# A hybrid encoder layer on one core: the opening in another order

## The chip, the core and the metric

The kernel runs on one core of a Trainium2 chip. The metric is the time of one execution on the device in microseconds (us), the median of several runs. A core has five engines with a queue each: PE (TensorE: matmuls and transposes, weight loads shown as PEld), DVE (VectorE), ACT (ScalarE), POOL (GpSimd) and SP (SyncE, which here issues all transfers). Each works its own list in order and waits on semaphores. PE writes into PSUM, eight banks of 128 x 512 floats, from which only DVE and ACT read here.

## The reference

One encoder layer on x of 1024 tokens by 1024 channels, conditioned by a vector c:

```
mod = silu(c) @ w_ada + b_ada          # six rows of 1024: sh1, sc1, gt1, sh2, sc2, gt2
h = rms_norm(x, g_norm1) * (1 + sc1) + sh1
qa, ka, va, qb, kb, vb, gates = split(h @ w_in)
o_a = neighbourhood_attention(rms_norm(qa), rms_norm(ka), va, rpb)        # 8 heads
o_b = merge of three dilated_window_attentions of rotary(rms_norm(qb)), rotary(rms_norm(kb)), vb
x = x + gt1 * ((sig(gate_a) * (o_a @ w_proj_a) + sig(gate_b) * (o_b @ w_proj_b)) @ w_o)
h2 = rms_norm(x, g_norm2) * (1 + sc2) + sh2
x = x + gt2 * ((silu(a) * up) @ w_ffn_out),   a, up = split(h2 @ w_ffn_in)
```

All data are float32. The change lies in the first two lines and the first part of the third.

## The kernel before, in words

**Split products.** A float32 matrix is kept as two parts, `hi` (rounded by an ACT copy, L101 for weights) and `lo` (the difference, on POOL or DVE, L102). A product is three matmuls, hi by hi, hi by lo and lo by hi (`PASS`). `wsplit` makes the two parts of a weight tile from a landed `raw` tile.

**The opening** (L142 to L729) has its order written out by hand for all engines: what stands first in the program goes first on each engine. It makes hT, the transposed and modulated h, in two parts of eight channel blocks k (128 channels each) by 1024 tokens, and the first six token tiles of the projection of unit 0. Its pieces:

- x is loaded in eight token tiles (L148, 512 KB each). `x_squares`, `x_rstd` and `x_scale` normalise tile t; for tiles 0 to 3 the scale sits in a diagonal matrix and `x_turn` transposes by a plain matmul (L207), for tiles 4 to 7 x itself is scaled and `x_turn` is a PE transpose (L209). Each `x_turn(t)` fills two PSUM banks, of the pair `d`, `v` or `s` by t modulo 3. `x_evac(t)` copies them to yT on DVE or ACT (L216, L218), as a table `XE` says.
- `load_block(k)` loads 1 MB of w_ada, the two columns blocks of sc1 and sh1 for channel block k, in two halves (`land`, L155); `unit_load(0, k)` loads unit 0's weights of block k (`raw`, L94). `start_load(k)` does both.
- `ada_rows(k)` multiplies c by that block on PE (L619) and asks for block k + 3 by `start_load(k + 3)`; `rowk[k]()` copies the row to SBUF on ACT (L625); `ada_turn(k)` turns it into columns on PE (L634); `ada_cols(k)` adds gains and biases on DVE (L639, L641).
- `h_half(k, hf)` makes one token half of block k of hT: a scale and shift on DVE (L647), hi on ACT (L648), lo on DVE (L651). With half 0 it also splits unit 0's weights of block k (`wsplit`, hi on ACT, lo on POOL).
- the loop at the end of the opening goes over k: `start_chunk(k, (0, 1, 2))` (nine matmuls, L656), `ada_turn`, `ada_cols` and both halves for block k + 2, `start_chunk(k, (3, 4, 5))`, then `ada_rows(k + 3)` and `rowk[k + 3]`.

Tables are asked for on SP's queue too: `rg` (L238) and the mask `bm` (L240) right behind x, then `cs` (L229) in `new_unit(0)`. From `rg` and `cs` POOL makes the rotary table `rtab` (L233, four operations), which stand on POOL ahead of the first weight split. Behind these, in the program, come the first three `start_load`.

**The main loop** goes over n, from 6 to 91; n = 8u + t is token tile t of unit u (of ten units, each a pair of heads). PE's order is by hand through the whole kernel; outside the opening a planner with a timeline of its own sets the order on the other engines. In iteration n PE does four of the tile's eight chunks (24 matmuls in all, L281), scores of attention items, products with v (`at_pv`, a `v` bank, copied by DVE at L476), turns (`qk_turn`: transposes of q and k, L339, with copies L357 to L360 on ACT and DVE), turns of the attention weights, and the other four chunks; for n below 10 all eight chunks come first. Then `proj_post` normalises q and k (ACT L299, L300; the copy of v at L316). The list `turns` says which tiles of unit 0 are turned in iterations 8 to 11; from 10 on, one tile of the tile two iterations before is turned as well. Turns of iterations 8 and 9 use the `s` banks, later ones the `v` banks. There are two banks of each kind.

The rest (gates, merge, output projection, feed-forward) isn't touched.

Of the kernel before, what the change touches and what calls it, by code (L numbers as in the profile page):

```python
# [35 lines left out]
def hybrid_layer(ctx: ExitStack, tc: tile.TileContext, x, colp, wada1, wada2, bada2, wqkv, wg, wpa, wpb,  # L36
# [21 lines left out]
    def bank(tag):  # L58
        return ps.tile([128, 512], F32, tag=tag, name="ps_" + tag)
# [29 lines left out]
    def fview(ap):  # L89
        return ap.bitcast(F32)  # L90
# [6 lines left out]
    def wsplit(r, eng=None):  # L97
        n = r.shape[1]
        hi = wp.tile([128, 512], F32R, tag="hi", bufs=NHL, name="whi")
        lo = wp.tile([128, 512], F32R, tag="lo", bufs=NHL, name="wlo")  # L100
        nc.scalar.activation(hi[:, :n], r, AF.Copy)  # L101
        (eng or nc.gpsimd).tensor_sub(lo[:, :n], r, fview(hi[:, :n]))  # L102
        return hi, lo
# [48 lines left out]
    def load_block(k):  # L152
        wblk[k] = [landing().rearrange("p (k n) -> p k n", k=4) for _ in range(2)]
        for hf in range(2):
            nc.sync.dma_start(wblk[k][hf], wada1[k, :, hf * 4:hf * 4 + 4, :])  # L155

    def unit_load(u, k):
        return wload(wqkv[u, :, k, :], 384)
# [3 lines left out]
    def start_load(k):  # L162
        if k < KT:
            load_block(k)
            raw0.append(unit_load(0, k))

    pw = bank("t")
    for i in range(WARM):
        nc.tensor.transpose(pw[:, :128], ident, ident)
# [2 lines left out]
    def x_squares(t):  # L172
        p, i = divmod(t, 2)
        if i == 0:
            ss2[p] = ap_.tile([128, 2], F32, tag="ss2", bufs=2, name="ss2")
        acc, junk = ss2[p][:, i:i + 1], hT[0][:, t, :]
        if XSQ[t] == "a":
            nc.scalar.activation(junk, xts[t], AF.Square, accum_out=acc)
        else:
            nc.vector.tensor_tensor_reduce(junk, xts[t], xts[t], 1.0, 0.0, ALU.mult, ALU.add, acc)  # L180
# [11 lines left out]
    def x_scale(t):  # L192

        r = xr[t // 2][:, t % 2:t % 2 + 1]
        if XSC[t] == "d":
            xd[t] = ap_.tile([128, 128], F32, tag="stg", bufs=3, name="xd")
            nc.vector.tensor_scalar(xd[t], ident, r, None, op0=ALU.mult)
        else:
            nc.vector.tensor_scalar(xts[t], xts[t], r, None, op0=ALU.mult)

    def x_turn(t):
        for g in range(2):
            pt = xp[t, g] = bank("dvs"[t % 3])
            for i in range(4):
                src, dst = xts[t][:, (g * 4 + i) * 128:(g * 4 + i + 1) * 128], pt[:, i * 128:(i + 1) * 128]
                if XSC[t] == "d":
                    nc.tensor.matmul(dst, src, xd[t], start=True, stop=True)  # L207
                else:
                    nc.tensor.transpose(dst, src, ident)  # L209

    def x_evac(t, gs=(0, 1)):
        for g in gs:
            dst = yT[g][:, :, t * 128:(t + 1) * 128]
            src = xp[t, g].rearrange("p (k q) -> p k q", k=4)
            if XE[t][g] == "v":
                nc.vector.tensor_copy(dst, src)  # L216
            else:
                nc.scalar.activation(dst, src, AF.Copy)  # L218
# [57 lines left out]
    def proj_chunk(U, t, k):  # L276
        if k == 0:
            U.pd[t] = bank("d" if U.u else "t")
        pd = U.pd[t]
        for i, (a, b) in enumerate(PASS):  # L280
            nc.tensor.matmul(pd[:, :384], tok(a, k, t), U.w[k][b][:, :384],  # L281
                             start=(k == 0 and i == 0), stop=(k == KT - 1 and i == 2))
# [321 lines left out]
    units = []  # L604
# [5 lines left out]
    rowk = {}  # L610

    def ada_rows(k):

        if k >= KT:
            return
        pa = bank("t")
        for kk in range(8):
            j = 32 * (kk % 4)
            nc.tensor.matmul(pa[j:j + 32, :256], c32[:, kk, :], wblk[k][kk // 4][:, kk % 4, :],  # L619
                             start=(kk < 4), stop=(kk >= 4))  # L620
        start_load(k + 3)

        def copy():
            rowk[k] = ap_.tile([128, 384], F32, tag="p", bufs=4, name="rowk")[:, :256]
            nc.scalar.activation(rowk[k], pa[:, :256], AF.Copy)  # L625

        rowk[k] = copy
# [3 lines left out]
    def ada_turn(k):  # L631
        ps_m = sck[k] = bank("t")
        for i in range(2):
            nc.tensor.matmul(ps_m[:, i:i + 1], rowk[k][:, i * 128:i * 128 + 128], ones, start=True, stop=True)  # L634

    def ada_cols(k):
        ps_m = sck[k]
        sc = sck[k] = ap_.tile([128, 2], F32, tag="sc", bufs=3, name="sc")
        nc.vector.scalar_tensor_tensor(sc[:, 0:1], ps_m[:, 0:1], g1_c[:, k:k + 1], bg1[:, k:k + 1],  # L639
                                       op0=ALU.mult, op1=ALU.add)  # L640
        nc.vector.tensor_add(sc[:, 1:2], ps_m[:, 1:2], bsh1[:, k:k + 1])  # L641

    def h_half(k, hf):
        sc = sck[k]
        hs = slice(hf * 512, hf * 512 + 512)
        y = yT[k // 4][:, k % 4, hs]
        nc.vector.tensor_scalar(y, y, sc[:, 0:1], sc[:, 1:2], op0=ALU.mult, op1=ALU.add)  # L647
        nc.scalar.activation(hT[0][:, k, hs], y, AF.Copy)  # L648
        if hf == 0:
            w0.append(wsplit(raw0[k]))  # L650
        nc.vector.tensor_sub(hT[1][:, k, hs], y, fview(hT[0][:, k, hs]))  # L651
# [4 lines left out]
                nc.tensor.matmul(U.pd[t][:, :384], tok(a, k, t), U.w[k][b][:, :384],  # L656
                                 start=(k == 0 and i == 0), stop=(k == KT - 1 and i == 2))

    for k in range(3):
        start_load(k)  # L660
    x_squares(0)
    x_squares(1)
    x_rstd(0)
# [9 lines left out]
    x_scale(3)  # L673
    x_turn(2)
    x_turn(3)
    ada_rows(0)
    x_squares(4)
    x_squares(5)
    x_evac(0, (1,))
# [8 lines left out]
    x_rstd(3)  # L688
    x_scale(6)
    x_scale(7)  # L690
    rowk[0]()
    x_evac(2)
    x_evac(3)
    x_turn(5)
    ada_turn(0)
    ada_rows(1)
    x_turn(6)
    x_evac(4)
    x_turn(7)
    rowk[1]()  # L700
    ada_cols(0)
    xp_.release()
    h1l = pool("h1l", "left")
    hT.append(h1l.tile([128, KT, S], F32R, name="hT1"))
    x_evac(5)
    h_half(0, 0)
    x_evac(6)
    x_evac(7)
    h_half(0, 1)
    ada_turn(1)  # L710
    ada_rows(2)
    ada_cols(1)
    h_half(1, 0)
    h_half(1, 1)
    rowk[2]()
    for tg, t in zip(["d", "d", "s", "s", "v", "v"], range(6)):
        U.pd[t] = bank(tg)
    for k in range(KT):
# [17 lines left out]
    for n in range(6, 92):  # L736
        u, t = divmod(n, 8)
        if u < 10:
            if t == 0:
                units.append(new_unit(u, [nextw[u, k] for k in range(KT)]))  # L740
            U = units[u]
            chunks = [lambda k=k, U=U, t=t: proj_chunk(U, t, k) for k in range(KT)]
        elif n - 80 < NPRE:
            chunks = gate_pre(n - 80)
        else:
            chunks = []
        if u + 1 < 10:
            for k in ([0, 1, 2, 3, 4, 5, 6, 7] if n == 6 else [t] if u else []):
                raws[u + 1, k] = unit_load(u + 1, k)
            if t == 6:  # L750
                for k in range(2):
                    nextw[u + 1, k] = wsplit(raws[u + 1, k])
        if t == 2 and 1 <= u <= 10:
            for slot, I in unit_items(units[u - 1]):
                ready.setdefault(8 * u + 2 + slot, []).append(I)
        if n == 8 * 7 + 5:
            combine_stats()
        ci = n - (8 * 7 + 7)
        if 0 <= ci < 12:
            combine_prep(ci)  # L760
        done, prev, cur = prev, cur, ready.pop(n, [])

        def chunk():
            if chunks:
                chunks.pop(0)()
                k = 8 - len(chunks)
                if t == 7 and u + 1 < 10 and k < 8 and k >= 2:
                    nextw[u + 1, k] = wsplit(raws[u + 1, k], nc.vector if k % 2 else None)

        turns = [(units[0], tt) for tt in {8: (0, 1, 2), 9: (3, 4, 5), 10: (6,), 11: (7,)}.get(n, ())]  # L770
        if 10 <= n <= 81:
            turns.append((units[(n - 2) // 8], (n - 2) % 8))
        chunk()
        chunk()
        chunk()
        chunk()
        if n < 10:
            while chunks:
                chunk()
        for I in cur:  # L780
            at_scores(I)
            at_qk(I, 0)
            at_qk(I, 1)
        for I in done:
            at_pv(I)
        for q in turns:
            qk_turn(*q, "s" if n < 10 else "v")
        for I in prev:
            at_turn(I, 0)
            at_turn(I, 1)  # L790
        chunk()
        chunk()
        chunk()
        chunk()
        if n >= 8 and (t != 7 or u > 8) and ada_state["i"] < 65:
            ada_step()
        if 1 <= ci < 13:
            combine_step(ci - 1)
        while chunks:
            chunk()  # L800
        if u < 10:
            proj_post(U, t)
# [516 lines left out]
```

## Time and profile before

| | us |
|---|---|
| median of 3 runs | 1610.39 |
| lowest and highest run | 1608.18 and 1611.52 |
| the profiled execution | 1611.13 |
| its span, first to last instruction | 1609.3 |

The span is what the profile divides: all times below count from its start. Of the profiled execution 1.8 us lie outside it. The mean granted TensorE clock was 0.984. The views used are the page (busy time by engine, the chain of work that ended last), the timeline of an engine (start, duration, engine, line, operation, tiles, count, and in brackets how long the engine had been idle and which work ended that), and the windows (busy time of each engine in given stretches, with clock and DMA).

### The profile page before, as it was taken

The numbers are of one execution on the slowest core, as the hardware profiler recorded it, in microseconds if no ns is written. First come the engines' busy times: TensorE is split into PE (matmuls) and PEld (weight loads), VectorE is DVE, ScalarE is ACT, GpSimd is POOL, SyncE is SP. The second block draws the span as 40 slices with busy tenths as digits, with TensorE's granted clock in tenths as the row PEclk, the third lists the DMA queues.
The fourth block names the chain that finished last, engine by engine and source line by source line (L and its number), as shares of the span: only waits on it lengthen the run. The fifth ranks groups of instructions, "written<-read, shape, count | busy, mean of one in ns | idle before, by whom it ended". The sixth has DMA issues, their size and how long they took to land.

```text
span 1609.3 us, 24779 instructions
## 1 busy us (share of the span) xinstructions
PE 1549.1 (96%) x8240; PEld 1293.8 (80%) x8240; DVE 1026.0 (64%) x2188; ACT 667.0 (41%) x1734; POOL 719.5 (45%) x672
## 2 busy tenths in 40 slices
PE   7989999999999999999999986999999999999997
PEld 6888888898888877878887775788888888888886
DVE  5666666776889843352437979866666666345476
ACT  5555555555545443512124533323233333344442
POOL 1332321221101040645425576867766666555565
PEclk8999999999999999999999998999999999999999
DMA  8332331344344351776645521333333333576774
GB/s 316 105 119 58 102 110 49 119 133 113 91 133 127 91 172 57 257 236 218 216 152 183 176 93 40 102 111 102 108 109 99 105 98 120 178 232 193 249 216 166
DMA packets 149056, 227.52 MB, mean 141 GB/s; under 512 B 27312, under 2 KB 65072, under 8 KB 148928
## 3 DMA queue, kind: packets, MB, share of 16 engines
q1 hardware_dynamic: 148928, 225.94, 44.1%
q8 instruction: 65, 1.06, 0.3%
q14 instruction: 63, 0.52, 0.1%
HBM read 172.28 MB, written 53.59 MB: 140 GB/s over the span
## 4 chain that ended last, share of the span: by engine, by line
PE 76%; DVE 11%; DMA 5%; issue 3%; ACT 2%; POOL 2%; SPq 0%; POOLq 0%; DVEq 0%; ACTq 0%
PE ps_d L281 14%; PE ps_t L1059 6%; PE ps_v L1059 6%; PE ps_s L1059 6%; PE ps_d L1059 6%; PE ps_d L570 4%; PE ps_d L592 4%; PE ps_s L570 4%; PE ps_d L1161 3%; PE ps_s L1161 3%; PE ps_v L473 2%; PE ps_s L432 2%; PE ps_v L1161 2%; PE ps_t L1161 2%; PE ps_t L570 2%
## 5 line engine op out<-in xcount | busy, mean ns | idle before, releaser
L102 POOL TENSOR_TENSOR wlo<-raw,whi 128x512 fp32r<-128x512 f32 (+2 forms) x269 | 362.2, 1354 | 474.9 <-ACT whi L101 455.4
L101 ACT ACTIVATE whi<-raw 128x512 fp32r<-128x512 f32 (+2 forms) x418 | 244.1, 604 | 431.3 <-DMA raw<-in_wg_dram 69.7
L281 PE MATMUL ps_d<-whi,hT 128*128 128x384 f32 x1152 | 317.9, 344 | 0.0
L102 DVE TENSOR_TENSOR wlo<-raw,whi 128x512 fp32r<-128x512 f32 (+1 forms) x149 | 150.5, 1019 | 129.0 <-ACT whi L101 114.9
L281 PEld LDWEIGHTS ps_d<-whi,hT 128*128 128x128 f32 x1152 | 211.2, 189 | 5.5 <-ACT vs L319 3.5
L281 PE MATMUL ps_d<-wlo,hT 128*128 128x384 f32 x576 | 194.2, 337 | 0.8 <-POOL wlo L102 0.8
L281 PEld LDWEIGHTS ps_d<-wlo,hT 128*128 128x128 f32 x576 | 108.9, 189 | 1.5 <-POOL wlo L102 1.5
L311 POOL TENSOR_TENSOR ra<-qn,rtab 128x64 f32<-128x64 f32 x48 | 16.5, 344 | 166.6 <-DVE qn L304 122.8
L996 POOL TENSOR_TENSOR c<-c 128x512 f32<-128x512 f32 x40 | 64.6, 1617 | 51.8 <-DVE c L1109 45.5
L101 ACT ACTIVATE whi<-ws 128x512 fp32r<-128x512 f32 x60 | 37.9, 632 | 117.1 <-DVE ws L1069 34.4
L447 ACT ACTIVATE P<-P,st 128x256 f32<-128x256 f32 (+2 forms) x100 | 46.3, 463 | 69.8 <-DVE st L446 69.8
L1059 PE MATMUL ps_t<-t,whi 128*128 128x512 f32 x160 | 52.6, 410 | 13.3 <-DVE c L995 12.1
L302 DVE TENSOR_REDUCE ss<-sq 128x4 f32<-128x256 f32 x80 | 33.2, 415 | 47.7 <-ACT sq L299 47.5
L447 ACT ACTIVATE P<-P,sx 128x384 f32<-128x384 f32 (+1 forms) x64 | 37.1, 580 | 51.6 <-DVE sx L446 51.6
L473 PE MATMUL ps_v<-PT,v 128*64 128x128 f32 (+1 forms) x672 | 55.0, 284 | 1.6 <-DVE PT L462 1.6
L458 PE MATMUL ps_t<-ident,P 128*128 128x128 f32 (+1 forms) x336 | 51.8, 275 | 4.3 <-DVE P L450 1.8
L432 PE MATMUL ps_s<-qk 64*128 64x256 f32 (+3 forms) x492 | 53.7, 321 | 2.2 <-DVE st L446 1.6
L592 PE MATMUL ps_d<-hT,whi 128*128 128x512 f32 x176 | 55.5, 396 | 0.0
L995 DVE TENSOR_TENSOR c<-c 128x512 f32<-128x512 f32 x40 | 45.5, 1139 | 14.2 <-ACT c L994 14.2
L570 PE MATMUL ps_s<-hT,whi 128*128 128x512 f32 x176 | 54.4, 390 | 0.0
L432 PEld LDWEIGHTS ps_s<-qk 64*128 64x128 f32 (+1 forms) x492 | 35.0, 182 | 24.0 <-issue 11.5
L876 DVE TENSOR_TENSOR raw<-raw 128x512 f32<-128x512 f32 x11 | 7.8, 708 | 70.9 <-DMA raw<-in_w_dram 51.4
(360 smaller groups left out, 4052.2 us busy)
## 6 DMA issues: line engine op xcount, KB each, us to landing
raw<-in_w_dram SPq DMA_DIRECT2D x165, 256.0 KB
ga_d<-c SPq DMA_DIRECT2D x77, 256.0 KB
raw<-ga_d SPq DMA_DIRECT2D x77, 256.0 KB
wa<-in_wada_dram SPq DMA_DIRECT2D x32, 512.0 KB
raw<-in_wqkv_dram SPq DMA_DIRECT2D x80, 192.0 KB
raw<-in_wo_dram SPq DMA_DIRECT2D x48, 256.0 KB
w_d<-raw SPq DMA_DIRECT2D x44, 256.0 KB
raw<-w_d SPq DMA_DIRECT2D x44, 256.0 KB
```

The source lines that it names most:

```text
L101: nc.scalar.activation(hi[:, :n], r, AF.Copy)
L102: (eng or nc.gpsimd).tensor_sub(lo[:, :n], r, fview(hi[:, :n]))
L281: nc.tensor.matmul(pd[:, :384], tok(a, k, t), U.w[k][b][:, :384], start=(k == 0 and i == 0), stop=(k == KT - 1 and i == 2))
L432: nc.tensor.matmul(I.pS[h][:nq, :nk], U.qk[a][hs, I.q0:I.q0 + nq], U.qk[2 + b][hs, I.kb0 * 128:I.kb0 * 128 + nk], start=(i == 0), stop=(i ...
L447: nc.scalar.activation(P[:nq, :nk], P[:nq, :nk], AF.Exp, scale=-1.0, bias=nm, accum_out=sm)
L458: nc.tensor.transpose(pt[:, i * 128:i * 128 + nq], P[:nq, i * 128:(i + 1) * 128], ident[:nq, :nq])
L473: nc.tensor.matmul(po[hs, :nq], U.v[:, I.kb0 + i, hs], I.PT[h][:, i, :nq], start=(i == 0), stop=(i == nkb - 1))
L570: nc.tensor.matmul(pb, wsl[a][:, j * 128:(j + 1) * 128], src[b][:, ksrc + j, hs], start=(done == 0 and j == 0 and i == 0), stop=(done + j ...
L592: nc.tensor.matmul(st["p"], gw[i, br][j][a][:, kk * 128:(kk + 1) * 128], hT[b][:, k, hs], start=(k == 0 and q == 0), stop=(k == 7 and q == 2))
L996: nc.gpsimd.tensor_mul(sg, sg, up) if j not in (0, HT) else nc.vector.tensor_mul(sg, sg, up)
L1059: nc.tensor.matmul(pb, w[p][:, k * 128:(k + 1) * 128], b[q][:, k], start=(k == 0 and i == 0), stop=(k == 3 and i == 2))
L1161: nc.tensor.matmul(pb[m], o[0][a][:, m * 128:(m + 1) * 128], o[1][b], start=(k == 0 and i == 0), stop=(k == HT - 1 and i == 2))
```

## The change

Three edits. The first three `start_load` move up, so that on SP's queue they stand right behind x, ahead of `rg`, `bm` and `cs`. In the opening's list `ada_rows(0)` and `rowk[0]` move behind `x_turn(5)` and the evictions of tiles 2 and 3; `rowk[1]` moves behind `h_half(0, 0)`; `h_half(0, 1)` moves behind `ada_rows(2)`, and `rowk[2]` right behind it, ahead of block 1. In the main loop the turns of unit 0 are spread over iterations 8 to 12, where they were in 8 to 11.

```diff
@@ -164,6 +164,8 @@
+    for k in range(3):
+        start_load(k)
     pw = bank("t")
     for i in range(WARM):
         nc.tensor.transpose(pw[:, :128], ident, ident)
@@ -656,8 +658,6 @@
-    for k in range(3):
-        start_load(k)
     x_squares(0)
@@ -673,7 +673,6 @@
     x_scale(3)
     x_turn(2)
     x_turn(3)
-    ada_rows(0)
     x_squares(4)
     x_squares(5)
     x_evac(0, (1,))
@@ -688,31 +687,32 @@
     x_rstd(3)
     x_scale(6)
     x_scale(7)
-    rowk[0]()
     x_evac(2)
     x_evac(3)
     x_turn(5)
+    ada_rows(0)
+    rowk[0]()
+    x_turn(6)
     ada_turn(0)
     ada_rows(1)
-    x_turn(6)
     x_evac(4)
     x_turn(7)
-    rowk[1]()
     ada_cols(0)
     xp_.release()
     h1l = pool("h1l", "left")
     hT.append(h1l.tile([128, KT, S], F32R, name="hT1"))
     x_evac(5)
     h_half(0, 0)
+    rowk[1]()
     x_evac(6)
     x_evac(7)
-    h_half(0, 1)
     ada_turn(1)
     ada_rows(2)
+    h_half(0, 1)
+    rowk[2]()
     ada_cols(1)
     h_half(1, 0)
     h_half(1, 1)
-    rowk[2]()
     for tg, t in zip(["d", "d", "s", "s", "v", "v"], range(6)):
         U.pd[t] = bank(tg)
@@ -767,7 +767,7 @@
-        turns = [(units[0], tt) for tt in {8: (0, 1, 2), 9: (3, 4, 5), 10: (6,), 11: (7,)}.get(n, ())]
+        turns = [(units[0], tt) for tt in {8: (0, 1, 2), 9: (3, 4), 10: (5,), 11: (6,), 12: (7,)}.get(n, ())]
         if 10 <= n <= 81:
             turns.append((units[(n - 2) // 8], (n - 2) % 8))
```

## The prediction

> **What bounds the kernel now.** I read the page first, for the engine that carries the time.
>
> ```profile
> PE 1549.1 (96%) x8240; PEld 1293.8 (80%) x8240; DVE 1026.0 (64%) x2188; ACT 667.0 (41%) x1734; POOL 719.5 (45%) x672
> ...
> PE 76%; DVE 11%; DMA 5%; issue 3%; ACT 2%; POOL 2%; SPq 0%; POOLq 0%; DVEq 0%; ACTq 0%
> ```
>
> PE is busy 96% of the span and makes 76% of the chain that ended last. A change of order adds and removes no work, so it can only win back time in which PE waits or runs slowly. The next view is PE's timeline of the opening (start, duration, engine, line, count, in brackets the idle time before and what ended it).
>
> ```profile
> 14.80 1.95 PE L207 MATMUL ps_d<-xd,xt 128*128 128x128 f32 x16
> 17.67 0.64 PE L619 MATMUL ps_t<-land,c 128*32 128x256 f32 x8 [0.93 <-DMA land<-in_wada_dram]
> 19.72 1.08 PE L619 MATMUL ps_t<-land,c 128*32 128x256 f32 x8 [1.41 <-DMA land<-in_wada_dram]
> 20.73 1.97 PE L209 MATMUL ps_v<-ident,xt 128*128 128x128 f32 x8
> ...
> 24.94 1.09 PE L209 MATMUL ps_d<-ident,xt 128*128 128x128 f32 x8
> 25.87 1.04 PE L209 MATMUL ps_v<-ident,xt 128*128 128x128 f32 x8
> ...
> 29.94 0.34 PE L656 MATMUL ps_s<-whi,hT 128*128 128x384 f32 x1
> 35.21 1.01 PE L634 MATMUL ps_t<-ones,rowk 128*128 128x1 f32 x4 [4.93 <-ACT rowk L625]
> ...
> 42.20 0.50 PE L634 MATMUL ps_t<-ones,rowk 128*128 128x1 f32 x4
> ...
> 47.13 0.61 PE L634 MATMUL ps_t<-ones,rowk 128*128 128x1 f32 x4
> ...
> 64.43 0.33 PE L656 MATMUL ps_d<-whi,hT 128*128 128x384 f32 x1
> ...
> 70.67 0.33 PE L281 MATMUL ps_t<-whi,hT 128*128 128x384 f32 x1
> ```
>
> The one long stall is the 4.93 us ahead of `ada_turn(2)` (35.21): PE waits for ACT's copy `rowk[2]` (L625). Before it, 2.3 us go in two waits of `ada_rows(0)` for its weights, with turns 4 to 7 queued behind them. From `ada_turn(3)` (42.20) to `ada_turn(4)` (47.13) the loop takes 4.93 us a step and PE hardly waits; so `ada_turn(3)` is my marker: what it gains, the rest inherits. Matmuls run at (70.67 - 64.43) / 36 = 0.173 us there.
>
> The windows view shows what a stall costs beyond itself (length, then busy time of PE, PEld, DVE, ACT, POOL; granted clock, DMA share, GB/s).
>
> ```profile
> 15.92:19.33 3.41, 1.47 (x16) 0.79 (x14) 3.20 (x9) 1.22 (x4) 1.71 (x4) 1.00 1.03 400
> 19.33:22.76 3.43, 3.04 (x18) 2.24 (x19) 1.25 (x3) 1.89 (x5) 0.00 (x0) 0.50 1.03 408
> ...
> 29.59:33.00 3.41, 0.69 (x4) 0.36 (x3) 2.04 (x5) 1.65 (x3) 0.15 (x1) 1.00 1.03 399
> 33.00:36.41 3.41, 1.20 (x5) 1.20 (x6) 2.06 (x5) 0.90 (x2) 0.94 (x1) 0.50 0.61 236
> 36.41:39.82 3.41, 3.41 (x17) 2.74 (x20) 2.52 (x5) 1.17 (x3) 1.10 (x1) 0.50 0.02 5
> ```
>
> A stretch of 3.4 us in which PE was busy 1.47 or 0.69 us is followed by clock 0.50, until a busy stretch has passed. That is why `ada_turn(2)` to `ada_turn(3)` took 7.0 us and the next step 4.93: 2.1 us are clock. The same windows show DMA full (share 1.03, 400 GB/s) to 33: in the opening a transfer moved ahead pushes another back.
>
> **The change, part by part.**
>
> *Row copies and evictions.* ACT, DVE and POOL in the opening:
>
> ```profile
> 34.79 0.37 ACT L625 ACTIVATE rowk<-ps_t 128x256 f32<-128x256 f32 x1
> ...
> 46.72 0.37 ACT L625 ACTIVATE rowk<-ps_t 128x256 f32<-128x256 f32 x1
> ```
> ```profile
> 31.15 0.55 DVE L647 TENSOR_SCALAR yT<-yT,sc 128x512 f32<-128x512 f32 x1
> ...
> 33.01 1.22 DVE L647 TENSOR_SCALAR yT<-yT,sc 128x512 f32<-128x512 f32 x1
> 34.92 0.69 DVE L651 TENSOR_TENSOR hT<-yT,hT 128x512 fp32r<-128x512 f32 x1 [0.69 <-ACT hT L648]
> ...
> 42.74 0.22 DVE L639 SCALAR_TENSOR_TENSOR sc<-ps_t,cp,bg 128x1 f32<-128x1 f32 x1 [1.69 <-PE ps_t L634]
> ...
> 96.59 0.28 DVE L446 CUSTOM_DVE_ANT_0 P<-ps_s,bmask 64x128 f32<-64x128 f32 x1
> ```
> ```profile
> 16.49 1.71 POOL L233 TENSOR_TENSOR rtab<-cs,rg 128x128 f32<-128x128 f32 x4 [15.19 <-DMA cs<-in_rope_dram]
> 27.44 1.12 POOL L102 TENSOR_TENSOR wlo<-raw,whi 128x384 fp32r<-128x384 f32 x1 [9.24 <-DMA land<-in_wada_dram]
> ```
>
> `rowk[2]` stood behind all of block 1's halves on ACT; now it stands behind `h_half(0, 1)`, long before its turn. So the 4.93 us wait goes, and the question is what is late next. Two routes lead to `ada_turn(3)`.
>
> Route A, over DVE and ACT. Turns 4 and 5 no longer wait behind `ada_rows(0)`. PE is free at 14.80 + 1.95 = 16.75; four turns at 1.09, `ada_rows(0)` and `(1)` at 1.08, `ada_turn(0)` at 0.50 make 7.0 us, so turn 7 ends near 23.8 instead of 25.87 + 1.04 = 26.91: 3.1 us earlier. I cost the moved evictions at nothing, since ACT and DVE do them while PE does these 7 us; without that cover, as now, turn 7 is 3.1 us later. What lies on DVE from turn 7 to the end of block 1 stays the same, so its end goes from 34.92 + 0.69 = 35.61 to 32.5. To this I add 0.7: `h_half(1, 0)` will now meet POOL, and this line takes 0.55 us alone (31.15) but 1.22 beside a split (33.01). So 33.2. From block 2's `ada_cols` through both halves, the row copy and to the turn is, from 42.74 to 47.13, 4.4 us. `ada_turn(3)` at 37.6.
>
> Route B, over the first weights. SP's queue now:
>
> ```profile
> 5.50 0.94 SPq L238 DMA_DIRECT2D rg<-in_ropeg_dram  x1
> 6.49 0.45 SPq L240 DMA_DIRECT2D bmask<-in_bmask_dram  x1
> 8.78 0.33 SPq L229 DMA_DIRECT2D cs<-in_rope_dram  x1
> 10.05 1.61 SPq L155 DMA_DIRECT2D land<-in_wada_dram  x2
> ...
> 17.65 0.33 SPq L94 DMA_DIRECT2D raw<-in_wqkv_dram  x1
> 19.69 0.92 SPq L155 DMA_DIRECT2D land<-in_wada_dram  x2
> ```
>
> Nine transfers (six `land` at 512 KB, three `raw` at 192 KB: 3.74 MB) pass `rg`, `bmask` and `cs` (416 KB). At 400 GB/s the weights gain 1.0 us, and the tables lose 9.3: `cs` lands at 25.8 instead of 16.49. The first block's second half came 3.2 us after `cs` (19.72), where 1.05 MB make 2.6, so I take 26.3. On POOL the four table operations stand ahead of the first `wlo`: 26.3 + 1.7 + 1.1 = 29.1, against 27.44 + 1.12 = 28.56 now. This is the wait that the change adds: queued behind it are all later splits, and PE, which can do one matmul of block 0 without `wlo`. From 29.1: eight matmuls at 0.173 = 1.4, so `ada_turn(2)` at 30.5, and 4.93 on to `ada_turn(3)` at 35.4. PE has then idled about 3.5 us, so I add half a window of slow clock, 1.7: 37.1. The mask itself is first used at 96.59; its lateness costs nothing, with 70 us of cover. `ada_rows(0)` takes block 3's loads along (issued at 19.69 now; the second half reuses a buffer that it reads). It ends no later than now, and block 3 is needed only after 30.5: nothing, unless they take over 11 us.
>
> The later route decides: 37.6 against 42.20, **4.6 us gained**. Ends: 5.3 (no meeting with POOL), and 3.1 (`cs` 2 us later, route B at 39.1).
>
> A page of the Trainium skill, "TensorE: Matmul & The Clock Gate" (Part 4, PE-mode transpose), speaks against this: it says that transposes don't count as busy work for the clock. By that rule the new stretch before `ada_rows(0)`, which holds little but transposes, would bring clock 0.50 on turns 6 and 7, and it is a rival below. The trace speaks against the rule: from 19.33 to 22.76 PE did 1.08 us of L619 and otherwise nearly only transposes, and at 22.76 the clock came back.
>
> *The turns of unit 0.* The stage around iterations 9 to 12, PE, ACT and DVE:
>
> ```profile
> 91.31 0.60 PE L339 MATMUL ps_s<-ident,qn 128*128 128x128 f32 x4
> 93.50 0.41 PE L339 MATMUL ps_s<-ident,qn 128*128 128x128 f32 x2 [1.58 <-POOL rb L313]
> ...
> 107.61 0.44 PE L339 MATMUL ps_v<-ident,qn 128*128 128x128 f32 x2
> ```
> ```profile
> 92.08 0.27 ACT L316 ACTIVATE v<-ps_d 128x128 f32<-128x128 f32 x1
> ```
> ```profile
> 108.14 0.22 DVE L476 COPY stg<-ps_v 128x64 f32<-128x64 f32 x1
> ```
>
> The third turn of iteration 9 waits 1.58 us; by the code it needs one of the two `s` banks back. Without it PE goes on to iteration 10 at 91.31 + 0.44 = 91.75, where it meets the next wait: its `d` bank is free when ACT has read `v`, at 92.35. It starts at 92.4 instead of 93.66: 1.3 gained. In iteration 12 there are now two turns beside `at_pv`, three users of two `v` banks, so the second turn waits for DVE's copy, which ended at 108.36, 0.75 after the one turn began: behind a first turn of 0.27 about 0.5 is lost. Net **0.8**; ends 1.3 gained and 0.5 lost, should the waits move on to `v` alone. The number of turns, copies and splits is the same.
>
> *Everything after.* Loads of the next unit wait for buffers, hence for work that moves along, so I carry the gain to the end. Outside the opening a planner orders all engines but PE, and may choose otherwise now. No row prices it; I take 0, and bounds of 2 us either way, near the 1.58 of a single such wait.
>
> Sum: 4.6 + 0.8 = 5.4 us. The profiled execution took 1611.13 (span 1609.3), so its like would take 1605.7; against the median of the runs, 1610.39, that is 1605.0.
>
> **Rivals.**
>
> *Transposes at half clock.* For it: a window with 1.47 us of PE work did bring 0.50, and 20.73 shows a turn at 1.97 us. Against it: turns 4 and 5 make that window busier, and the return at 22.76. Price: work of 19.33 to 22.76 takes twice as long, 1.7 us on turn 7 and so on route A: 39.3, gain 2.9 + 0.8 = 3.7, 1606.7.
>
> *The tables land late and eat the gain.* For it: DMA is full, and three more blocks are issued behind the tables. Against it: landings have followed the order of issue. Each us that `cs` comes later is a us on route B. At 30.3, `wlo` ends at 33.1, `ada_turn(3)` comes at 41.1: gain 1.1 + 0.8, 1608.5. That is also how the change would fail to do what it says: one wait of PE for another.
>
> *The planner gives back more, slower.* Of the chain 24% (386 us) is not PE, and it lies where the planner sets order on ACT, DVE and POOL: splits and evictions that PE waits for. With the turns shifted, every later place can fall differently. Point from which it decides: 2.3% more of these 386 us, 8.9 us, turns -5.4 into +3.5: 1613.9. Against it: the iterations past 12 keep their turns.
>
> **How the numbers follow.** A measurement of this kernel tells about 0.2% (3.2 us) from no change. Chances: forecast 0.55 (own range 1602 to 1607: opening 3.1 to 5.3, turns -0.5 to 1.3, planner 2 either way, the ends not all together), half-clock transposes 0.11 (1606.7, still faster), late tables 0.18 (1608.5, same), planner 0.16 (1613.9, slower). So faster 0.66, same 0.18, slower 0.16. The range reaches from 1602 over the late tables to 1611, and leaves out the planner's case and 0.04 below.
>
> **What would show it.** Right: no wait over 1 us ahead of the third `ada_turn`; turn 7 ending near 24; the table operations on POOL near 26 to 28, with PE's one long wait now ending on `wlo` near 29; `ada_turn(3)` near 37.6 and then steps of 4.9 to 5.1; no wait among the turns of iteration 9, and one of half a us at iteration 12. Wrong: `rtab` past 30, a clock of 0.50 from 19 to 23, a first `ada_turn` of the loop still waiting for `rowk`, or a marker that gains while the end doesn't, which would put the loss on the planner's stretch.

## The result, and the profile after

The changed kernel takes 1604.28 us, median of 20 runs (1602.06 to 1610.44); the kernel before takes 1610.04 beside it (20 runs, 1605.66 to 1617.24). The ratio is 0.9972, with a 95% interval of 0.9960 to 0.9984: 2.6 to 6.4 us faster. The prediction, 1605.0 with a range of 1602 to 1611, held. The profiled execution of the changed kernel has a span of 1603.6 us against 1609.3. In the changed kernel lines 167 to 660 stand two lower: L211 is the `x_turn` that was L209, L621 `ada_rows`, L627 `rowk`, L636 `ada_turn`, L658 `start_chunk`.

The page after, busy time of the engines:

```profile
PE 1542.5 (96%) x8240; PEld 1289.0 (80%) x8240; DVE 1026.6 (64%) x2188; ACT 667.1 (42%) x1734; POOL 717.3 (45%) x672
```

The counts of instructions are those of before. PE is busy 6.6 us less with the same work: it works less at half clock (the mean granted clock is 0.989, against 0.984). Where, the timeline of PE in the opening after says (start, duration, engine, line, count, in brackets the idle time before and what ended it):

```profile
18.32 1.07 PE L621 MATMUL ps_t<-land,c 128*32 128x256 f32 x16
...
22.10 1.09 PE L211 MATMUL ps_v<-ident,xt 128*128 128x128 f32 x8
...
25.22 0.44 PE L658 MATMUL ps_d<-whi,hT 128*128 128x384 f32 x1
29.76 0.69 PE L658 MATMUL ps_d<-wlo,hT 128*128 128x384 f32 x1 [4.10 <-POOL wlo L102]
...
32.49 0.85 PE L636 MATMUL ps_t<-ones,rowk 128*128 128x1 f32 x4
...
37.77 0.61 PE L636 MATMUL ps_t<-ones,rowk 128*128 128x1 f32 x4
...
42.81 0.60 PE L636 MATMUL ps_t<-ones,rowk 128*128 128x1 f32 x4
...
57.99 0.61 PE L636 MATMUL ps_t<-ones,rowk 128*128 128x1 f32 x4
```

The turns no longer wait behind the weights: `ada_rows(0)` does both its halves in one go at 18.32, and turn 7 ends at 23.19 where it ended at 26.91. The stall of 4.93 us ahead of `ada_turn(2)` is gone, and one of 4.10 us stands ahead of the first matmul with `wlo`. `ada_turn(3)` comes at 37.77 instead of 42.20, and the loop goes on at 5.04 a step; the last `ada_turn` is at 57.99, where before has it at 62.31:

```profile
62.31 0.61 PE L634 MATMUL ps_t<-ones,rowk 128*128 128x1 f32 x4
```

So, between these two profiles, 4.4 us are won by the marker, and 4.3 by the end of the opening.

The windows view after (length, busy time of PE, PEld, DVE, ACT, POOL; granted clock, DMA share, GB/s) shows the new place of the stall:

```profile
15.92:19.33 3.41, 3.41 (x40) 2.62 (x38) 3.20 (x9) 2.67 (x8) 0.00 (x0) 1.00 1.04 411
19.33:22.76 3.43, 3.23 (x38) 2.32 (x35) 1.58 (x5) 2.36 (x6) 0.00 (x0) 1.00 1.01 400
22.76:26.17 3.41, 2.56 (x25) 1.21 (x23) 2.44 (x4) 1.61 (x5) 0.00 (x0) 1.00 1.07 393
26.17:29.59 3.42, 0.00 (x0) 0.00 (x0) 2.35 (x5) 1.62 (x4) 3.17 (x5) 0.55 1.03 400
29.59:33.00 3.41, 3.24 (x12) 3.24 (x12) 2.51 (x3) 0.63 (x1) 1.53 (x2) 0.50 1.01 389
33.00:36.41 3.41, 3.41 (x29) 2.58 (x30) 2.30 (x5) 1.04 (x2) 1.02 (x1) 0.95 0.59 228
```

The first two rows are nearly full of PE work at clock 1.00, where before the second was at 0.50. The half clock now lies from about 26.5 (0.55 as a mean of 1.00 and 0.50 puts its start there) to 33.3, in good part on a PE that has nothing to do. Before, it lay from 33.00 to 39.82, for its second half on a PE that was busy without a break.

What holds the first `wlo` is read off POOL's timeline after:

```profile
26.42 2.33 POOL L235 TENSOR_TENSOR rtab<-cs,rg 128x128 f32<-128x128 f32 x4 [25.12 <-DMA cs<-in_rope_dram]
28.72 2.40 POOL L102 TENSOR_TENSOR wlo<-raw,whi 128x384 fp32r<-128x384 f32 x2
```

The four table operations stand ahead of the split, and `cs` now lands near 26.4, with the weights asked for ahead of it. Then the turns of unit 0, PE after:

```profile
87.06 0.60 PE L341 MATMUL ps_s<-ident,qn 128*128 128x128 f32 x4
88.14 0.44 PE L283 MATMUL ps_d<-whi,hT 128*128 128x384 f32 x1 [0.48 <-ACT v L318]
...
90.43 0.39 PE L434 MATMUL ps_s<-qk 64*64 64x128 f32 x6
...
102.99 0.41 PE L341 MATMUL ps_v<-ident,qn 128*128 128x128 f32 x2 [0.46 <-DVE stg L478]
...
107.97 0.62 PE L434 MATMUL ps_s<-qk 64*128 64x256 f32 x6
```

The wait of 1.58 for a bank is gone, and a wait of 0.46 stands in iteration 12. The scores of iterations 10 and 13 stood in before at

```profile
95.95 0.39 PE L432 MATMUL ps_s<-qk 64*64 64x128 f32 x6
...
112.61 0.62 PE L432 MATMUL ps_s<-qk 64*128 64x256 f32 x6
```

Against the same work of before (91.31, 95.95 and 112.61) the rows at 87.06, 90.43 and 107.97 stand 4.25, 5.52 and 4.64 earlier.

### The profile page after: what moved, and what is told of

Its sections match the earlier page's. It is cut to its first block, busy times and chain, and to the rows that moved or that the text cites. A ratio compares the mean times of both kernels' runs of the same rounds, so it can differ in the third digit from the quotient of the medians.

```text
span 1603.6 us, 24772 instructions
## 1 busy us (share of the span) xinstructions
PE 1542.5 (96%) x8240; PEld 1289.0 (80%) x8240; DVE 1026.6 (64%) x2188; ACT 667.1 (42%) x1734; POOL 717.3 (45%) x672
## 4 chain that ended last, share of the span: by engine, by line
PE 75%; DVE 12%; DMA 6%; issue 3%; ACT 2%; POOL 2%; SPq 0%; POOLq 0%; DVEq 0%; ACTq 0%
PE ps_d L283 14%; PE ps_t L1059 6%; PE ps_s L1059 6%; PE ps_v L1059 6%; PE ps_d L1059 6%; PE ps_d L594 4%; PE ps_s L572 3%; PE ps_d L572 3%; PE ps_s L1161 3%; PE ps_d L1161 3%; PE ps_v L475 2%; PE ps_s L434 2%; PE ps_v L1161 2%; PE ps_t L1161 2%; PE ps_t L572 2%
## 5 line engine op out<-in xcount | busy, mean ns | idle before, releaser
L304 DVE TENSOR_REDUCE ss<-sq 128x4 f32<-128x256 f32 x80 | 33.2, 415 | 45.9 <-ACT sq L301 45.8
L460 PE MATMUL ps_t<-ident,P 128*128 128x128 f32 (+1 forms) x336 | 51.6, 274 | 4.5 <-DVE P L452 1.9
L448 DVE CUSTOM_DVE_ANT_0 P<-ps_s,rb 128x384 f32<-128x384 f32 (+1 forms) x64 | 31.3, 517 | 33.7 <-PE ps_s L434 33.7
```

The costliest lines, as they stand in the source:

```text
L460: nc.tensor.transpose(pt[:, i * 128:i * 128 + nq], P[:nq, i * 128:(i + 1) * 128], ident[:nq, :nq])
```

## The experiments

The question was what the 4.4 us at the marker are made of, since the result shows one stall replaced by another of nearly the same length. **My theory** was the prediction's: `ada_turn(3)` is set by the route over DVE and ACT, which the new order shortens by taking the turns ahead of `ada_rows(0)` and the row copies ahead of the halves; early weights are worth 1 us of landing and cost nothing. **Rivals**: that the early weights carry the gain; that the late rotary table costs part of it; that the clock, not any wait, makes the difference.

All marks below are PE's starts of `ada_turn`, in one profile each; ratios are against the kernel before on the same chip.

| run | ratio (95%) | median us | `ada_turn` (2), (3), (4) | last |
|---|---|---|---|---|
| before | | | 35.21, 42.20, 47.13 | 62.31 |
| changed | 0.9972 (0.9960 to 0.9984) | 1604.28 | 32.49, 37.77, 42.81 | 57.99 |
| e1 turns alone | 0.9993 (0.9980 to 1.0007) | 1607.38 | 36.99, 44.48, 49.41 | 64.59 |
| e2 without weights first | 0.9988 (0.9974 to 1.0002) | 1606.94 | 28.02, 37.34, 45.31 | 60.38 |
| e3 weights first alone | 0.9993 (0.9979 to 1.0008) | 1608.07 | 33.16, 40.50, 45.43 | 60.61 |
| e4 tables second | 0.9984 (0.9969 to 1.0000) | 1605.89 | 27.81, 37.20, 45.02 | 60.09 |
| e5 changed, stall filled | 0.9965 (0.9949 to 0.9981) | 1603.88 | 31.56, 37.39, 42.43 | 57.60 |
| e6 = e4, stall filled | 0.9976 (0.9962 to 0.9990) | 1605.35 | 27.94, 37.34, 42.38 | 57.55 |
| e7 changed, halves in pairs | 0.9965 (0.9948 to 0.9981) | 1605.29 | 32.95, 38.78, 43.56 | 57.90 |
| e8 = e4, halves in pairs | 0.9953 (0.9934 to 0.9972) | 1601.88 | 27.62, 34.22, 40.68 | 55.02 |
| e9 = e8, stall filled | 0.9955 (0.9938 to 0.9972) | 1601.41 | 27.66, 34.34, 39.22 | 53.56 |
| e10 = e5 with transposes | one run | 1600.55 | 31.74, 37.59, 42.63 | 57.81 |
| e11 changed, once more | one run | 1611.49 | 32.84, 38.90, 43.83 | 59.01 |

No interval in this table is clear of the changed kernel's, so what follows on the parts of the gain rests on the marks and clocks of the profiles.

**e1_turns_only**: the kernel before with the turns edit alone.

```diff
-... {8: (0, 1, 2), 9: (3, 4, 5), 10: (6,), 11: (7,)} ...
+... {8: (0, 1, 2), 9: (3, 4), 10: (5,), 11: (6,), 12: (7,)} ...
```

> The kernel before with only the turns of unit 0 spread over iterations 8 to 12. Theory: the wait of 1.58 us at the third turn of iteration 9 goes, the scores of the first attention item start 1.27 us earlier (95.95 in before, 94.7 here), but the moved turn brings its own 0.4 us and a wait of 0.46 us into iteration 12, so the scores of iteration 13 (112.61 in before) come only 0.4 us earlier, 112.2; time 0.9995 to 1.0 of before, not to be told from it. Rival, the term of the prediction: 0.8 us left at iteration 13 (111.8).

In time it can't be told from before. Its marks all stand late, since the first block of w_ada landed late in this profile; PE's timeline of e1:

```profile
19.23 1.08 PE L619 MATMUL ps_t<-land,c 128*32 128x256 f32 x8 [2.50 <-DMA land<-in_wada_dram]
...
94.81 0.45 PE L281 MATMUL ps_d<-whi,hT 128*128 128x384 f32 x1 [0.48 <-ACT v L316]
...
109.70 0.41 PE L339 MATMUL ps_v<-ident,qn 128*128 128x128 f32 x2 [0.46 <-DVE stg L476]
```

So absolute marks missed what was expected, and only distances within the run count: from the last `ada_turn` to the scores of iteration 13 it is 50.10 us, where before has 112.61 - 62.31 = 50.30. The waits are those of the changed kernel, 0.48 and 0.46. The edit is worth 0.2 us here and 0.4 in the changed kernel, not 0.8. The later profiles agree: over this stretch the changed kernel, e5, e6 and e10, which have the edit and full clock there, take 49.98 to 50.13, and e3, without the edit, 50.44. The opening of e1 is that of before, so it also shows how far a mark can move with the landings alone: its last `ada_turn` is 2.28 later.

**e2_no_weights_first**: the changed kernel with the first three `start_load` back behind the tables, so copies and turns alone.

```diff
-    for k in range(3):
-        start_load(k)
     pw = bank("t")
...
+    for k in range(3):
+        start_load(k)
     x_squares(0)
```

> The changed kernel with the first three start_load put back behind the tables. Theory: the order of row copies and evictions made the gain and the early weights give almost nothing, since the route over DVE and ACT decides: PE's wait of 4.1 us on the first wlo goes, ada_turn(3) comes at 37 to 38 (37.77 in the changed kernel, 42.20 in before), with a PE wait of about 4 us ahead of it, half clock behind it and ada_turn(4) at 43 to 44 (42.81). Time 0.9965 to 0.9985 of before. Rival: the early weights carry a good part of the gain; then ada_turn(3) comes at 39 or later and the time is 0.9985 or more.

PE's timeline and windows of e2:

```profile
28.02 0.53 PE L634 MATMUL ps_t<-ones,rowk 128*128 128x1 f32 x4
...
37.34 1.02 PE L634 MATMUL ps_t<-ones,rowk 128*128 128x1 f32 x4 [4.24 <-ACT rowk L625]
...
45.31 0.50 PE L634 MATMUL ps_t<-ones,rowk 128*128 128x1 f32 x4
```
```profile
36.41:39.82 3.41, 2.48 (x9) 2.48 (x10) 1.52 (x4) 1.40 (x3) 0.00 (x0) 0.62 0.55 213
39.82:43.23 3.41, 3.41 (x22) 1.71 (x20) 2.53 (x3) 1.15 (x3) 1.09 (x1) 0.50 0.00 0
43.23:46.64 3.41, 3.41 (x23) 3.40 (x20) 0.75 (x3) 0.39 (x1) 0.00 (x0) 0.88 0.81 244
```

The wait for `wlo` is gone, `ada_turn(2)` is 4.5 us earlier than in the changed kernel, and `ada_turn(3)` still comes at 37.34: DVE and ACT set it, as the prediction said. But PE gets there early, idles for 4.24 us, and the half clock starts as the stall ends (about 37.2, to 44.05). PE then has its row work and matmuls to do at half speed, and `ada_turn(4)` comes 7.97 us later instead of 5. I had expected 43 to 44 for it, one stretch of half clock; it was two. At that mark e2 is 1.8 us ahead of before, where the changed kernel is 4.3 ahead.

**e3_weights_only**: the kernel before with the three `start_load` early and nothing else (the first hunk of the diff, and the second).

> The kernel before with only the first three start_load ahead of the tables. Theory: the wait for rowk[2] ahead of ada_turn(2) stays and ends at 34 to 35 (35.21 in before), ada_turn(3) at 41 to 42; time 0.9990 to 1.0005 of before. Rival: weights that land 1 us earlier move everything, ada_turn(3) at 40 or earlier and time 0.9985 or less.

PE's timeline of e3:

```profile
29.40 0.69 PE L658 MATMUL ps_d<-wlo,hT 128*128 128x384 f32 x1 [3.85 <-POOL wlo L102]
...
33.16 1.01 PE L636 MATMUL ps_t<-ones,rowk 128*128 128x1 f32 x4 [0.82 <-ACT rowk L627]
```

The wait for `wlo` is that of the changed kernel, and it takes the place of most of the wait for `rowk[2]`, of which 0.82 are left. `ada_turn(3)` came at 40.50, earlier than the 41 to 42 expected: 1.7 us ahead of before. That is less than half of the gain, and less than the 2.28 between before and e1, and the time can't be told from before: what early weights do by themselves is not shown.

**e4_tables_second**: the changed kernel with `rg` and `cs` asked for behind block 0, ahead of blocks 1 and 2. If the late table cost time, this would win it.

```diff
-    for k in range(3):
-        start_load(k)
+    start_load(0)
+    rg = ...; nc.sync.dma_start(rg, ropeg)
+    cs0 = ...; nc.sync.dma_start(cs0, rope)
+    start_load(1)
+    start_load(2)
```

> The changed kernel with the two rotary tables (160 KB) asked for behind the first block of weights instead of behind the third; the mask stays behind. Theory: the rotary table on POOL is made before the first split, the wait of 4.1 us on wlo goes and DVE isn't slowed by POOL in the same stretch: ada_turn(3) at 36.5 to 37, 1 us earlier than in the changed kernel; but PE then waits at that turn, its clock falls to 0.50 behind it, and ada_turn(4) comes at 42 to 43 (42.81). Time 0.996 to 0.998 of before, within 1 us of the changed kernel. Rival: the wait on wlo bounds the opening; then ada_turn(4) comes at 40 or earlier and the time falls by 3 us more, to 0.9955 or less.

PE's timeline of e4:

```profile
37.20 1.01 PE L638 MATMUL ps_t<-ones,rowk 128*128 128x1 f32 x4 [4.24 <-ACT rowk L629]
...
45.02 0.50 PE L638 MATMUL ps_t<-ones,rowk 128*128 128x1 f32 x4
```

It looks like e2, not like an improved changed kernel. Taking PE's early wait away only moved the stall to `ada_turn(3)`, and half clock (to about 43.6) took the loop's next step. I had expected 42 to 43 for `ada_turn(4)`. The theory that early weights cost nothing and bring 1 us falls here, by the marks (the times don't separate e4 from the changed kernel): **what they bring is the place of the stall**. PE has to wait for DVE in any case; waiting at `wlo`, near 26, it has the half clock behind it when it is needed again.

**e5_filler** and **e6_tables_filler** test that, by keeping the clock up through the stall: 16 products of the identity with itself, written into columns of a PSUM bank that nothing reads. They are extra work and change nothing else. In e5 they stand in the changed kernel ahead of the loop, in the wait for `wlo`; in e6 in the kernel of e4, ahead of `ada_turn(3)`.

```diff
+    for i in range(16):
+        nc.tensor.matmul(U.pd[5][:, 384:512], ident, ident, start=True, stop=True)
     for k in range(KT):
```
```diff
     def ada_turn(k):
         ps_m = sck[k] = bank("t")
+        for i in range(16 if k == 3 else 0):
+            nc.tensor.matmul(ps_m[:, 128:256], ident, ident, start=True, stop=True)
```

> The changed kernel with 16 idle matmuls (128 columns of the identity, into a bank that is overwritten later) on PE in the 4.1 us in which it waits for the first wlo. Theory: one stall of 4 to 5 us with the half clock behind it is in every version, and what counts is where it stands; here the clock stays at 1.00 from 26 to 34 us, ada_turn(2) comes at 31.2 instead of 32.49, DVE no longer waits for it, and ada_turn(3) and ada_turn(4) come 0.6 us earlier than in the changed kernel (37.77 and 42.81). Time within 1 us of the changed kernel, 0.996 to 0.9975 of before. Rival: the clock behind the stall has no part in it, or the filler delays PE; then ada_turn(3) stays at 37.7 or comes later.

> The kernel of e4_tables_second with 16 idle matmuls on PE in the 4.2 us in which it waits ahead of ada_turn(3). Theory (place of the stall and clock): the clock stays at 1.00 from 37 to 44 us, ada_turn(3) stays at 37.2 and ada_turn(4) comes at 42.2 instead of 45.02, the last ada_turn at 57.3 instead of 60.09: 2.8 us less than e4_tables_second, time 0.996 to 0.9975 of before. Rival (the weights in front are worth their 2 us by landing early, or the splits are late): ada_turn(4) stays at 44 or later.

PE's timeline of e6, and its windows:

```profile
33.30 3.84 PE L638 MATMUL ps_t<-ident 128*128 128x128 f32 x32 [0.18 <-DVE sc L647]
37.34 0.60 PE L640 MATMUL ps_t<-ones,rowk 128*128 128x1 f32 x4 [0.20 <-ACT rowk L629]
...
42.38 0.61 PE L640 MATMUL ps_t<-ones,rowk 128*128 128x1 f32 x4
```
```profile
33.00:36.41 3.41, 3.23 (x28) 3.11 (x28) 2.62 (x6) 1.07 (x3) 1.09 (x1) 1.00 1.03 400
36.41:39.82 3.41, 3.21 (x28) 2.68 (x30) 1.79 (x5) 1.82 (x4) 0.00 (x0) 1.00 0.65 253
```

With the stall filled, `ada_turn(3)` is where it was (37.34 against 37.20), the clock stays at 1.00, and `ada_turn(4)` comes at 42.38 instead of 45.02. Up to `ada_turn(3)` the marks of e4 and e6 agree to 0.15 us, and the program behind it is the same, so the 2.64 us are the clock's. In time they don't show (medians 1605.89 and 1605.35). In e5 the same filling brings 0.4 (42.43 against 42.81), and 1.4 against the second profile of the changed kernel (43.83 in e11): there the half clock costs less. Both end their opening at the same place, 57.6, with the stall at different places; with DVE as it is, no order tried gave more.

**e7_pair**, **e8_tables_pair** and **e9_pair_filler** go for DVE, which sets 37.3 and the step of 5.04. DVE's timeline after, block 2:

```profile
33.37 0.22 DVE L641 SCALAR_TENSOR_TENSOR sc<-ps_t,cp,bg 128x1 f32<-128x1 f32 x1 [0.58 <-PE ps_t L636]
...
33.69 0.55 DVE L649 TENSOR_SCALAR yT<-yT,sc 128x512 f32<-128x512 f32 x1
34.94 0.69 DVE L653 TENSOR_TENSOR hT<-yT,hT 128x512 fp32r<-128x512 f32 x1 [0.70 <-ACT hT L650]
35.54 1.23 DVE L649 TENSOR_SCALAR yT<-yT,sc 128x512 f32<-128x512 f32 x1
37.48 0.69 DVE L653 TENSOR_TENSOR hT<-yT,hT 128x512 fp32r<-128x512 f32 x1 [0.70 <-ACT hT L650]
```

Twice a block DVE waits 0.70 us for ACT's copy, between the scale of a half and its lo. `h_pair` does both scales first, for blocks 1 and up; e7 is this in the changed kernel, e8 in that of e4, and e9 adds six idle products ahead of `ada_turn(3)` to e8, as e6 does.

```diff
+    def h_pair(k):
+        ...
+        for y in ys:
+            nc.vector.tensor_scalar(y, y, sc[:, 0:1], sc[:, 1:2], op0=ALU.mult, op1=ALU.add)
+        nc.scalar.activation(hT[0][:, k, hv[0]], ys[0], AF.Copy)
+        w0.append(wsplit(raw0[k]))
+        nc.scalar.activation(hT[0][:, k, hv[1]], ys[1], AF.Copy)
+        for y, hs in zip(ys, hv):
+            nc.vector.tensor_sub(hT[1][:, k, hs], y, fview(hT[0][:, k, hs]))
...
-    h_half(1, 0)
-    h_half(1, 1)
+    h_pair(1)
...
-            h_half(k + 2, 0)
-            h_half(k + 2, 1)
+            h_pair(k + 2)
```

> The changed kernel with both halves of a block from block 1 on scaled ahead of the two lo subtractions on DVE, so that DVE doesn't wait 0.7 us twice a block for ACT's hi. Theory: the loop's 5.04 us a step is the round of ada_cols, two halves, row copy and turn, while PE has 4.65 us of work a step; the step falls to 4.65 to 4.85, ada_turn(3) comes at 36 to 36.5 and the last ada_turn at 54.5 to 56 (57.99 in the changed kernel): 2 to 3.5 us less, time 0.995 to 0.9965 of before. Rival: PE is the bound of the loop already; the step stays at 5.0.

> The kernel of e4_tables_second with the same pairing of halves. Theory: the stall ahead of ada_turn(3) shrinks from 4.24 us to 1.5 to 2.5, too little for the clock to fall, and no other takes its place, so ada_turn(3) comes at 35 to 36, ada_turn(4) at 40 to 41 (42.81 in the changed kernel) and the last one at 54 to 55.5; time 0.9945 to 0.9965 of before, the best so far. Rival: the stall is still long enough for the half clock and ada_turn(4) comes at 43 or later.

> The kernel of e8_tables_pair with 6 idle matmuls on PE in the 1.5 us in which it waits ahead of ada_turn(3). Theory: the fall of the clock to 0.50 behind that wait (35.4 to 38.7 us) goes, ada_turn(3) stays at 34.2, ada_turn(4) comes at 39.0 instead of 40.68 and the last one at 53.4 instead of 55.02; time 0.994 to 0.9955 of before. Rival: so short a wait doesn't cost the clock, or the clock falls elsewhere; the last ada_turn stays at 55.

PE's timeline of e8, and its windows:

```profile
34.22 0.60 PE L638 MATMUL ps_t<-ones,rowk 128*128 128x1 f32 x4 [1.51 <-ACT rowk L629]
...
40.68 0.50 PE L638 MATMUL ps_t<-ones,rowk 128*128 128x1 f32 x4
45.46 0.50 PE L638 MATMUL ps_t<-ones,rowk 128*128 128x1 f32 x4
```
```profile
33.00:36.41 3.41, 2.19 (x11) 2.20 (x12) 3.04 (x6) 1.68 (x4) 1.09 (x1) 0.83 1.03 401
36.41:39.82 3.41, 3.41 (x25) 1.92 (x24) 1.86 (x2) 1.43 (x4) 1.10 (x1) 0.67 0.59 221
```

The step falls to 4.78 in all three, with PE busy throughout. In the changed kernel (e7) that helps little, since there PE is held by the late `wlo` and the half clock: the last `ada_turn` is at 57.90. With the tables second (e8) `ada_turn(3)` is at 34.22, and the last one at 55.02, 3.0 ahead of the changed kernel. By the marks, then, the late table is no loss while DVE is slow, and one as soon as DVE is not. In e8 the clock still falls behind the wait of 1.51; in e9, with that wait filled, the window from 33.00 to 36.41 has PE busy for 3.22 us, the clock stays at 1.00, and `ada_turn(4)` comes at 39.22 instead of 40.68, as expected. e8 and e9 have the lowest medians of all kernels that ran several times, 1601.88 and 1601.41, and ratios of 0.9953 and 0.9955; both beat the kernel before clearly. Their intervals overlap with that of the changed kernel, so the last 2 to 3 us over it are likely and not settled. e9's 1.5 us over e8 at the mark don't show in the time.

**e10_transposes**: e5 with 28 PE transposes of the identity in place of the 16 products.

```diff
-    for i in range(16):
-        nc.tensor.matmul(U.pd[5][:, 384:512], ident, ident, start=True, stop=True)
+    for i in range(28):
+        nc.tensor.transpose(U.pd[5][:, 384:512], ident, ident)
```

> The kernel of e5_filler with 28 PE transposes of the identity in place of the 16 idle matmuls. If transposes count as busy work for the clock, it stays at 1.00 from 26 to 34 us and ada_turn(3) comes at 37.3; if they don't (the rival of the prediction), the clock falls to 0.50 within 3.4 us of their start, as in the changed kernel, ada_turn(2) comes at 32.5 and ada_turn(3) at 37.8.

PE's timeline of e10, and its windows:

```profile
25.61 3.27 PE L719 MATMUL ps_v<-ident 128*128 128x128 f32 x28
...
30.24 0.44 PE L658 MATMUL ps_d<-wlo,hT 128*128 128x384 f32 x1 [1.18 <-POOL wlo L102]
```
```profile
26.17:29.59 3.42, 2.89 (x26) 2.63 (x24) 1.97 (x4) 1.55 (x4) 2.71 (x5) 1.00 1.04 401
29.59:33.00 3.41, 2.76 (x17) 2.77 (x18) 2.70 (x3) 1.03 (x2) 2.02 (x2) 1.00 1.03 328
```

Transposes alone keep the clock at 1.00 through the stall, where it fell to 0.50 in all four profiles that have this wait unfilled (changed, e3, e7 and e11); `ada_turn(3)` and `(4)` come at 37.59 and 42.63, 0.2 behind e5, and the one run took 1600.55 us. The Trainium skill, "TensorE: Matmul & The Clock Gate", Part 4 (PE-mode transpose), says that they don't count as busy work for the clock; for these float32 transposes the measurement says otherwise, and it decides.

**e11_changed_again**: the changed kernel once more, unaltered, for the spread of the marks.

> The changed kernel again, for the spread of the marks between profiled executions: every theory expects ada_turn(3) at 37.8 and the last ada_turn at 58.0; by the shift of the opening that e1_turns_only showed against before (2.3 us by later landings), up to 2 us off.

Windows of e11:

```profile
26.17:29.59 3.42, 0.00 (x0) 0.00 (x0) 2.18 (x5) 1.79 (x4) 2.92 (x5) 0.88 1.03 400
29.59:33.00 3.41, 2.88 (x10) 2.89 (x10) 2.71 (x3) 0.63 (x1) 1.89 (x2) 0.50 1.02 392
33.00:36.41 3.41, 3.41 (x18) 3.13 (x20) 2.10 (x6) 1.04 (x2) 0.67 (x1) 0.62 0.61 236
```

The stall is the same (4.30 us, `wlo` at 30.12), but the half clock starts at about 28.8 instead of 26.5, and lasts to 35.6. `ada_turn(3)` comes at 38.90, and the last one at 59.01: 1.1 and 1.0 later than in the first profile. So a mark of one profile is good to about 1 us where a half clock lies ahead of it, and to 2.3 where the first weights land late, as in e1. The 4.4 us at the marker is a difference of two profiles: with the opening of e1 for before, or e11 for the changed kernel, it would be 3.3 to 6.7. The 2.6 us between e4 and e6 stand above this, since the marks ahead of them agree; sums of parts below 1 us don't.

## Why the prediction was right

**Route A**: turn 7 at 23.8 (measured 23.19), DVE's end of block 1 at 33.2 (32.79), `ada_turn(3)` at 37.6 (37.77; in e2, e5 and e6, where PE doesn't hold it, 37.3 to 37.4). Right as a bound, and e2 shows the route: with `ada_turn(2)` at 28.02, `ada_turn(3)` doesn't come before 37.34.

**Route B**: `cs` at 26.3 (26.4), the first `wlo` at 29.1 (PE takes it at 29.76, since the four table operations took 2.33 us and not 1.7), `ada_turn(2)` at 30.5 and up to 1.7 more for the clock (32.49). Right to 0.7 us. I took route A as the later one by 0.5; in the changed kernel DVE, done at 32.79, waited 0.58 for `ada_turn(2)` (33.37), so route B came last, by 0.4 at the marker (37.77 against 37.3 to 37.4). In e11, with the half clock later, by more: 38.90. That 4.6 was so near to 4.4 is in part luck: the route that I named didn't decide, but the two lay within half a us of each other.

**The clock** I had priced as an amount, half a window of 1.7 us on route B. That size was right and the view too narrow: the price of a stall depends on what PE has to do in the 3.4 or 6.8 us after its fall, and I didn't ask that of the order without early weights. My working gave the early weights 1.0 us of landing; e2 and e4 show that without them, or with the tables ahead of two of them, `ada_turn(4)` would stand at 45.0 to 45.3 and not at 42.8. By it, e2 and e4 would have been at least as fast as the changed kernel. The sum came out right since the wait for `wlo` was in it, as a cost that happened to be covered.

**The turns of unit 0**: the term that was mis-sized. "Net 0.8" measured 0.4: the gain was 1.27 (predicted 1.3), from -4.25 at 87.06 to -5.52 at 90.43; the loss in iteration 12 was 0.88, not 0.5. Of it 0.46 are the wait, as predicted. The rest is the turn's own time: it left iteration 9, where I counted its leaving within the 1.3, and came back in iteration 12, where I didn't count it.

**Everything after**: taken as nothing. From 110 us on the instructions of every engine stand in the same order in both traces, so the planner's case doesn't hold. Yet the distance between the two traces runs from 2.6 to 6.5 us over the rest of the span and is 5.7 at its end, 1.1 more than at iteration 13; the second profile of the changed kernel has a span of 1609.7, 6.1 longer than the first. Of these 6.1 us, 2.45 are there by iteration 13 (110.42): 1.0 from the opening, and 1.4 from a half clock in iteration 8 that the first profile doesn't have (last section). The rest is variation from run to run whose cause I didn't find; the ratio over 20 runs, 4.5 us with 2.6 to 6.4, is the better measure, and the marks (4.6 at iteration 13) agree with it.

**The rivals.** Transposes at half clock: the windows from 15.92 to 22.76, about half of whose PE time is transposes, stand at 1.00, which alone decides little; e10 tests it by itself, and there the clock stayed up. Late tables: `cs` landed at 26.4, not past 30; e4, which has it early, is no faster. They are late enough to hold PE, which was worked out on route B. The kernel does what the change says, and one wait of PE did take the place of another, yet at a cheaper place.

**What stays open.** In the first profile the clock fell about 0.85 us after PE ran dry at 25.66. The row from 22.76 to 26.17 shows PE busy for 2.56 of 3.41 us, with short transposes and the narrow matmuls of `ada_rows` and `ada_turn`; how much of these counts for the clock, no run took apart.

## What to carry over

When PE has to wait for another engine in any case, the wait itself may cost nothing, but the half clock behind it does: look in the windows at what PE does in the next 3.4 to 6.8 us (10.2 in e3), and let it wait where another engine still sets the pace, or fill the wait with idle products (worth 2.6 us at the next mark in one order, 0.4 in the other, and not seen in the time of either). A transfer that lands earlier may gain nothing, and one that lands later may cost nothing; ask which wait comes last once it has moved. A turn or copy that is taken out of one iteration has to be paid for in another, with its own time and not its waits alone.

## What the runs showed of the hardware

- The half clock came in whole stretches. With a mean between 1.00 and 0.50 read as a share of the window, it lasted 6.83 us after the change (26.51 to 33.34), 6.83 in e11 (28.77 to 35.60), 6.82 in e2 (37.23 to 44.05) and in e4, 3.41 in e8 (35.25 to 38.66), and 10.24 in e3 (28.22 to 38.46): one, two or three times 3.41. When it begins differs from run to run. That agrees with the Trainium skill, "TensorE: Matmul & The Clock Gate", Part 1, which tells of a free-running window of 3413 ns and of two states, half and full clock.
- The same wait can cost a window of half clock or nothing. Ahead of the third turn of iteration 8 PE waits 1.7 us in all thirteen profiles. In e2, e4, e8 and e11 the clock fell there a second time, at 85.0, 84.6, 79.6 and 83.4, for 3.41 us, and the stretch from the last `ada_turn` to iteration 13 took 51.4 to 51.6 us, where the others with the turns edit have 49.8 to 50.1. These falls lie 14, 14, 13 and 16 times 3.41 us behind the first fall of the same run. In the 3.41 us just ahead of them PE was busy for 1.58 to 1.70; in before, e1, e3, e7 and the changed kernel, counted from their own first fall in the same way, the stretch with most of this wait had 1.70 to 1.95, and the clock stayed. So it seems to be the place of the wait among these stretches that decides; no run set out to test it.
- A fall needs no long gap. In e8 a wait of 1.51 us, with PE busy for 2.19 of the 3.41 us around it, was followed by 0.50. The Trainium skill, "TensorE: Matmul & The Clock Gate", asks in its table of advice (Why this matters for your kernels) for no gaps over about 3 us; here that wasn't enough.
- DVE's scale of 128x512 took 0.55 us beside an idle POOL and 1.22 to 1.23 beside a weight split on it, as in the kernel before; new is that the lo subtraction, 0.69 alone, took 0.92 beside the rotary table (26.51 in the trace after) and 1.12 beside two splits (29.14).
